# Row-wise infinity norm of an 8192x8192 matrix: the last 128 results transposed on VectorE and stored in four runs of 128 bytes

## The chip, the core and the metric

One core of a Trainium2 chip runs the kernel; the other seven stay idle. The metric is the device time of one execution in microseconds (us). The kernel before takes 626.61 us, the median of three runs that lie between 626.55 and 626.79.

Three parts of the core matter here. **DVE** (VectorE) computes the maxima. **SP** (SyncE) and **ACT** (ScalarE) do nothing but issue DMAs, each into a hardware queue of its own; 16 DMA engines carry the data of both. **POOL** (GpSimd) closes the program: it waits for the last transfers and resets the semaphores.

## What is computed

```python
x = randn(8192, 8192)                          # float32, 268 MB
out = np.linalg.norm(x, ord=np.inf, axis=1)    # 8192 float32
```

For a matrix, `ord=np.inf` with `axis=1` is the largest absolute value of each row. So every element is read once from HBM, and 32 KB are written.

## The kernel before, in words

The 8192 rows are 64 rows for each of the 128 partitions: 40 "bulk" rows and 24 "tail" rows.

**Bulk (L261 to L269).** 20 loads of 8 MB on SP, each two rows (16,384 elements) per partition, into a ring of three slots. One reduction on DVE per load writes two columns of `r_bulk`. A load waits until DVE has read the slot that it overwrites.

**Tail (L272 to L317).** Row r of the tail in partition p is DRAM row `split + 24 p + r` (`x_t`, L241), so 24 results lie side by side in each partition's output. The 24 rows are cut into 37 loads (`TAIL`, L20) that shrink from 16,384 to 512 elements per partition. A load may end inside a row. Then DVE reduces that piece to a partial maximum, which is put into a slot just ahead of the place in the ring where the row's last piece will land; the reduction of the last piece reads those slots with it (L307 to L313: `slot`, `frm`), and writes the row's column of `r_tail`. So the final reduction of a row depends on the reductions of all its pieces. The helper `absmax` (L252) records every reduction, so that all have line L253 in the profile.

The two last rows, 22 and 23, are loaded in alternation in 15 pieces (from the 22nd entry of `TAIL` on). The five last loads of the program are, in order: j = 32, a piece of row 23 (640 elements); j = 33, of row 22 (640); j = 34, of row 23 (512); j = 35, the last piece of row 22 (512); j = 36, the last piece of row 23 (512). Rows 22 and 23 have seven partials each, so that their final reductions read 519 elements.

**Stores.** When the reduction of load j = 34 is done (L314), ACT issues the store of `r_bulk` (L316): 640 runs of 32 bytes. After the last reduction SP issues the store of `r_tail` (L318): for each partition one run of 24 floats, 128 runs of 96 bytes in all.

**Order and waits.** The tile framework keeps the order of the code on each engine and adds semaphore waits. DVE counts its finished instructions in one semaphore; each DMA reports on one of eight semaphores ("lanes"), used in turn. `drop_implied_waits` (L134) takes away waits that others imply. An instruction that keeps two waits has the first of them in a small wait instruction of its own, ahead of it in the same queue. `finish_on_pool` (L71) rewrites the end: all engines meet at a barrier; POOL waits for the other lanes, clears the semaphores around the last store's lane, and then waits for that lane. Nothing of the program comes after that.

Of the kernel before, what the change touches and what calls it, by code (L numbers as in the profile page):

```python
# [12 lines left out]
F32 = mybir.dt.float32  # L13
# [3 lines left out]

HEAD, STEP = 32, 8

TAIL = [  # L20
# [10 lines left out]
]  # L31

# [178 lines left out]
@with_exitstack  # L211
def kernel(
    ctx: ExitStack,
    tc: tile.TileContext,
    x: bass.AP,
    out: bass.AP,
    G: int = 4,
    B: int = 2,
    SLOTS: int = 3,
    PAD: int = 128,  # L220
):
    nc = tc.nc
    P = nc.NUM_PARTITIONS
    rows, cols = x.shape
    W = B * cols
    R = SLOTS * W + PAD * 4


    n_tail = sum(w for _, w in TAIL) // cols
    met = 0  # L230
    for lo, w in sorted(TAIL):
        assert lo == met
        met += w
    assert met == n_tail * cols
    n_bulk_rows = rows // P - n_tail
    assert n_bulk_rows % (G * B) == 0
    A = n_bulk_rows // (G * B)
    split = n_bulk_rows * P
    x_b = x[:split].rearrange("(a p n b) c -> a n p (b c)", p=P, a=A, n=G, b=B)
    out_b = out[:split].rearrange("(a p n b) -> p a (n b)", p=P, a=A, n=G, b=B)  # L240
    x_t = x[split:].rearrange("(p t) c -> p (t c)", p=P)  # L241
    out_t = out[split:].rearrange("(p t) -> p t", p=P)

    pool = ctx.enter_context(tc.tile_pool(name="sbuf", bufs=1))
    r_bulk = pool.tile([P, A, G * B], F32)
    r_tail = pool.tile([P, n_tail], F32)
    used = [HEAD, A * G * B, n_tail]
    gap = -sum(-(-n // STEP) * STEP for n in used) % PAD
    pool.tile([P, gap], F32, name="gap")
    ring = pool.tile([P, R], F32)  # L250

    def absmax(o, i):  # L252
        return nc.vector.reduce_max(  # L253
            out=o, in_=i, axis=X, apply_absolute_value=True
        )

    def after(ins, first, kind):
        info = mybir.DependencyInfo(kind, mybir.DependencyReason.SCHED_ONLY)
        tc.add_manual_dep(ins.ins, first.ins.name, info, reason="order")

    for a in range(A):  # L261
        for n in range(G):
            at = (a * G + n) % SLOTS * W
            t = ring[:, at : at + W]
            nc.sync.dma_start(out=t, in_=x_b[a, n])
            absmax(
                r_bulk[:, a, n * B : (n + 1) * B],
                t.rearrange("p (b c) -> p b c", b=B),
            )  # L269


    pieces = []  # L272
    for j, (at, w) in enumerate(TAIL):
        end = at + w
        while at < end:
            r = at // cols
            to = min(end, (r + 1) * cols)
            pieces.append((j, r, to - at))
            at = to
    of_row = [[k for k, s in enumerate(pieces) if s[1] == r] for r in range(n_tail)]  # L280


    here = A * G % SLOTS * W
    start, slot = [], []
    for j, (_, w) in enumerate(TAIL):
        first = next(s for s in pieces if s[0] == j)
        ks = of_row[first[1]]
        n_part = len(ks) - 1 if pieces[ks[-1]][0] == j else 0
        at = -(-(here + n_part) // PAD) * PAD
        if at + w > R:  # L290
            at = -(-n_part // PAD) * PAD
        start.append(at)
        slot.append(at - n_part)
        here = at + w

    for j, (src, w) in enumerate(TAIL):
        at = start[j]
        nc.sync.dma_start(out=ring[:, at : at + w], in_=x_t[:, src : src + w])
        here = [k for k, s in enumerate(pieces) if s[0] == j]
        offs = [at + sum(pieces[i][2] for i in here[:m]) for m in range(len(here))]  # L300
        todo = list(zip(here, offs))
        if slot[j] != at:

            todo = todo[1:] + todo[:1]
        for k, lo in todo:
            _, r, n = pieces[k]
            ks = of_row[r]  # L307
            if k == ks[-1]:
                frm = slot[j] if len(ks) > 1 else lo
                done = absmax(r_tail[:, r : r + 1], ring[:, frm : lo + n])  # L310
            else:
                to = slot[pieces[ks[-1]][0]] + ks.index(k)
                done = absmax(ring[:, to : to + 1], ring[:, lo : lo + n])  # L313
        if j == len(TAIL) - 3:  # L314

            ins = nc.scalar.dma_start(out=out_b, in_=r_bulk[:])  # L316
            after(ins, done, mybir.DependencyClass.Sync)  # L317
    nc.sync.dma_start(out=out_t, in_=r_tail[:])  # L318
    nc.at_finalize(drop_implied_waits)
    nc.at_finalize(start_first_load_early)  # L320
    nc.at_finalize(finish_on_pool)
    nc.at_finalize(open_without_vector)
# [30 lines left out]
```

## Time and profile before

| | |
|---|---|
| median of three runs | 626.61 us (626.55 to 626.79) |
| the profiled execution's own time | 626.65 us |
| its span, first to last instruction of the program | 624.0 us |
| what lies around the span | 2.65 us |
| DVE busy | 553.1 us, 89% of the span |
| bytes read from HBM | 268.44 MB, mean 430 GB/s over the span |

How to read it: the span runs from the first instruction of the program to the last that an engine's instruction stream holds. A DMA that lands after that lies outside the span but inside the execution's time. "Busy" counts computing instructions alone; SP and ACT only issue DMAs and so have no busy time. In the chain, "issue" is time in which an engine waited for nothing that the profile shows, and a name with q (SPq, DVEq) is the sequencer of that engine, which waits, branches and issues DMAs.

### The profile page before, as it was taken

How to read it: one execution, taken by the hardware profiler on the slowest of the kernel's cores; microseconds unless marked ns; L12 is line 12 of the kernel's file. 1: busy time of each engine (PE TensorE's matmuls, PEld its weight loads, DVE VectorE, ACT ScalarE, POOL GpSimd, SP SyncE). 2: the span in 40 equal slices, each digit the busy share in tenths (PEclk: the TensorE clock that was granted, in tenths of full speed). 3: DMA queues.
4: the chain of work that ended last, by engine and by line, in shares of the span. 5: the costliest groups of instructions: out<-in, count | busy, mean ns of one | idle time of the engine just before them, and what ended most of it. 6: DMA issues, size and time to landing. Idle time of an engine off the chain costs nothing.

```text
span 624.0 us, 166 instructions
## 1 busy us (share of the span) xinstructions
DVE 553.1 (89%) x76; POOL 0.2 (0%) x4
## 2 busy tenths in 40 slices
DVE  0588988889988899888898888988899999999999
POOL 0000000000000000000000000000000000000000
DMA  9999999999999999999999999999999999999998
GB/s 403 454 420 454 420 441 433 408 466 403 471 403 454 420 454 420 450 424 429 445 408 466 403 466 408 454 420 454 409 435 445 422 436 428 429 427 431 429 425 343
DMA packets 8865, 268.47 MB, mean 430 GB/s; under 512 B 1568, under 2 KB 1568, under 8 KB 3488
## 3 DMA queue, kind: packets, MB, share of 16 engines
q1 hardware_dynamic: 8208, 268.44, 99.7%
q10 hardware_dynamic: 656, 0.02, 0.1%
q14 instruction: 1, 0.01, 0.0%
HBM read 268.44 MB, written 0.03 MB: 430 GB/s over the span
## 4 chain that ended last, share of the span: by engine, by line
DMA 61%; DVE 38%; issue 0%; DVEq 0%
DMA ring<-in_x_dram 61%; DVE r_bulk L253 19%; DVE ring L253 10%; DVE r_tail L253 9%; DVEq L348 0%
## 5 line engine op out<-in xcount | busy, mean ns | idle before, releaser
L253 DVE TENSOR_REDUCE r_bulk<-ring 128x2 f32<-128x16384 f32 x20 | 344.4, 17220 | 62.1 <-DMA ring<-in_x_dram 62.1
L253 DVE TENSOR_REDUCE r_tail<-ring 128x1 f32<-128x8192 f32 (+14 forms) x24 | 109.7, 4587 | 7.7 <-DMA ring<-in_x_dram 7.7
L253 DVE TENSOR_REDUCE ring<-ring 128x1 f32<-128x5248 f32 (+26 forms) x32 | 101.5, 3215 | 0.2 <-DMA ring<-in_x_dram 0.2
L337 POOL MEMSET const-bfloat16-1.0<- 128x1 bf16 x1 | 0.1, 101 | 0.0
L337 POOL MEMSET const-uint8-127<- 128x1 uint8 x1 | 0.1, 101 | 0.0
L337 POOL MEMSET const-float32-0.0<- 128x1 f32 x1 | 0.1, 98 | 0.2 <-issue 0.2
L337 POOL MEMSET const-float32-1.0<- 128x1 f32 x1 | 0.1, 98 | 0.0
## 6 DMA issues: line engine op xcount, KB each, us to landing
ring<-in_x_dram SPq DMA_DIRECT2D x1, 7744.0 KB, 39.6
ring<-in_x_dram SPq DMA_DIRECT2D x1, 7168.0 KB, 37.2
ring<-in_x_dram SPq DMA_DIRECT2D x1, 6400.0 KB, 33.0
ring<-in_x_dram SPq DMA_DIRECT2D x1, 5696.0 KB, 36.7
ring<-in_x_dram SPq DMA_DIRECT2D x1, 5056.0 KB, 41.0
ring<-in_x_dram SPq DMA_DIRECT2D x1, 4544.0 KB, 36.0
ring<-in_x_dram SPq DMA_DIRECT2D x1, 4032.0 KB, 31.9
ring<-in_x_dram SPq DMA_DIRECT2D x1, 3648.0 KB, 40.2
```

What stands on the lines that cost most here:

```text
L253: return nc.vector.reduce_max(out=o, in_=i, axis=X, apply_absolute_value=True)
L337: nc = _bacc.Bacc("TRN2", target_bir_lowering=False, num_devices=1)
```

## The change

All results now lie in one tile `r_all` of 64 columns: 40 of the bulk, then 24 of the tail. `r_bulk` and `r_tail` are views of it.

The last tail row (23) is no longer one of 24 adjacent rows per partition. It takes the last 128 rows of the matrix, one per partition (`x_l`, `out_l`); the other 23 tail rows are now 23 adjacent rows per partition. The loads of row 23 read from `x_l`, those of the others from `x_t` with 23 rows per partition.

The entries j = 34 and j = 35 of `TAIL` change places: first the last piece of row 22 (so row 22 is complete), then a piece of row 23; the last load, j = 36, stays.

The store of `r_bulk` on ACT is tied to the reduction of j = 33 instead of j = 34. A new store on ACT follows it: 23 tail columns, 128 runs of 92 bytes, once j = 34 has completed row 22.

After the last reduction DVE transposes columns 32 to 63 of `r_all`: each block of 32 partitions by 32 columns for itself. Column 63, the results of the last row, so becomes partitions 31, 63, 95 and 127 of `turned`, each with 32 results side by side. SP stores these four partitions: four runs of 128 bytes.

```diff
-    (194944, 640), (187264, 640), (195584, 512), (187904, 512),
+    (194944, 640), (187264, 640), (187904, 512), (195584, 512),
     (196096, 512),
...
-    x_t = x[split:].rearrange("(p t) c -> p (t c)", p=P)
-    out_t = out[split:].rearrange("(p t) -> p t", p=P)
+    n_lane = n_tail - 1
+    last = rows - P
+    x_t = x[split:last].rearrange("(p t) c -> p (t c)", p=P)
+    x_l = x[last:]
+    out_t = out[split:last].rearrange("(p t) -> p t", p=P)
+    out_l = out[last:].rearrange("(q i) -> q i", i=SQ)
...
-    r_bulk = pool.tile([P, A, G * B], F32)
-    r_tail = pool.tile([P, n_tail], F32)
-    used = [HEAD, A * G * B, n_tail]
+    n_bulk = A * G * B
+    assert n_bulk + n_tail >= SQ
+    r_all = pool.tile([P, n_bulk + n_tail], F32)
+    turned = pool.tile([P, SQ], F32)
+    r_bulk = r_all[:, :n_bulk].rearrange("p (a k) -> p a k", a=A)
+    r_tail = r_all[:, n_bulk:]
+    used = [HEAD, n_bulk + n_tail, SQ]
...
-        nc.sync.dma_start(out=ring[:, at : at + w], in_=x_t[:, src : src + w])
+        of, lo = (x_l, src - n_lane * cols) if src >= n_lane * cols else (x_t, src)
+        nc.sync.dma_start(out=ring[:, at : at + w], in_=of[:, lo : lo + w])
...
-        if j == len(TAIL) - 3:
-
-            ins = nc.scalar.dma_start(out=out_b, in_=r_bulk[:])
-            after(ins, done, mybir.DependencyClass.Sync)
-    nc.sync.dma_start(out=out_t, in_=r_tail[:])
+        if j == len(TAIL) - 4:
+
+            ins = nc.scalar.dma_start(out=out_b, in_=r_bulk)
+            after(ins, done, mybir.DependencyClass.Sync)
+        if j == len(TAIL) - 3:
+            nc.scalar.dma_start(out=out_t, in_=r_tail[:, :n_lane])
+    nc.vector.transpose(out=turned[:], in_=r_all[:, n_bulk + n_tail - SQ :])
+    nc.sync.dma_start(out=out_l, in_=turned[SQ - 1 :: SQ, :])
```

(`SQ` is 32.)

More of the change, by code (lines that the diff above doesn't have):

```diff
@@ L18 @@
 HEAD, STEP = 32, 8
+SQ = 32
 TAIL = [
```

## The prediction

> **What bounds the kernel now.** I read the page first, for the engines' shares and the chain.
>
> ```profile
> DVE 553.1 (89%) x76; POOL 0.2 (0%) x4
> ...
> DMA 61%; DVE 38%; issue 0%; DVEq 0%
> ```
>
> Loads and reductions share the chain, and only the stage at the end tells which of them a change there meets. So I read the end of the chain of waits (start, length, what):
>
> ```profile
> 533.82 39.07 DMA ring<-in_x_dram
> 572.89 0.02 issue
> 572.92 10.08 DVE ring L253 x2
> ...
> 606.33 15.17 DVE ring L253 x13
> 621.50 0.45 issue
> 621.95 0.14 DVE r_tail L253
> 622.09 0.36 issue
> 622.45 0.78 DVEq L348
> ```
>
> The last load that DVE waited for landed at 572.89. From there on reduction follows reduction: DVE is the bound for the last 50 us, and an instruction added there adds its whole cadence. But loads are close behind. By the trace's landings, the last ten loads land 0.14 to 0.27 us before their reductions start (the last at 622.41, its reduction starts at 622.55). So DVE could not gain much, and what delays DVE costs in full.
>
> The timeline has the last instructions, and the windows what the DMAs did meanwhile (length, DVE busy, POOL busy, clock, DMA share, GB/s):
>
> ```profile
> 621.36 0.68 DVE L253 TENSOR_REDUCE ring<-ring 128x1 f32<-128x512 f32 x1
> 621.95 0.68 DVE L253 TENSOR_REDUCE r_tail<-ring 128x1 f32<-128x519 f32 x1
> 622.55 0.68 DVE L253 TENSOR_REDUCE r_tail<-ring 128x1 f32<-128x519 f32 x1
> 622.07 0.41 ACTq L316 DMA_DIRECT2D out_dram<-r_bulk  x1
> 623.26 0.35 SPq L318 DMA_DIRECT2D out_dram<-r_tail  x1
> ```
> ```profile
> 621.00:622.00 1.00, 1.00 (x3) 0.00 (x0) 1.00 0.30 115
> 622.00:623.00 1.00, 1.00 (x3) 0.00 (x0) 1.00 0.01 2
> 623.00:624.00 1.00, 0.23 (x1) 0.00 (x0) 1.00 0.32 21
> 624.00:625.00 1.00, 0.00 (x0) 0.00 (x0) 1.00 0.09 12
> ```
>
> Each reduction starts 0.08 us before the end of the one before it (621.36 + 0.68 = 622.04 against 621.95). DVE ends at 623.23, SP issues the last store 0.03 later, and its packets move after 624. The view of DMA issues tells when stores land, in us from the issue:
>
> ```profile
> out_dram<-r_bulk ACTq DMA_DIRECT2D x1, 20.0 KB, 1.9
> out_dram<-r_tail SPq DMA_DIRECT2D x1, 12.0 KB, 1.4
> ```
>
> So the last store lands at 623.26 + 1.43 = 624.70, after the span's end (624.0), and POOL's last wait is for it. The profiled execution took 626.65 us, 0.04 above the median 626.61; from the landing to its end, with what lies ahead of the span, is 1.95 us, which I leave as it is. Three terms remain.
>
> **Term 1: two new waits of DVE on itself.** In the old order j = 34 was a piece of row 23 and j = 35 the end of row 22, so that each final reduction needed partials no younger than the reduction two places ahead. After the swap j = 34 completes row 22 and reads the partial that j = 33, just ahead, has written; j = 36 reads that of j = 35. The trace of before has no reduction that waits for its direct predecessor; I bound the cost. DVE's counter rises 0.01 us after an instruction's end, where the follower now starts 0.08 before it: at least 0.09 each. These reductions have two waits, so the counter's wait stands in an instruction of its own. In before such a one ran 0.028 us after its count (621.450, 621.478) and took 0.021; with 0.03 more for the start of the reduction (572.89 landed, 572.92 started, in the chain), the follower starts 0.01 + 0.03 + 0.02 + 0.03 = 0.09 after the predecessor's end instead of 0.08 ahead of it: 0.17 each. As the upper end I take 0.30 each: the fixed part of a reduction by a line through two rows,
>
> ```profile
> L253 DVE TENSOR_REDUCE ring<-ring 128x1 f32<-128x128 f32 x1 | 0.3, 275 | 0.0
> L253 DVE TENSOR_REDUCE r_tail<-ring 128x1 f32<-128x519 f32 x2 | 1.3, 683 | 0.0
> ```
>
> is 275 - 128 x (683 - 275)/391 = 141 ns, and it could be laid bare on top of the wait. Term 1: **+0.35** (0.18 to 0.60). Queued behind the waits on DVE are j = 35, j = 36 and the transpose; for the last of them waits SP's last store alone. Nothing hides it: the last load, landed at 622.41, is early already.
>
> The Trainium skill speaks against this term: "VectorE: DVE Perf Modes", section "The DRAIN you can't avoid", says that eight copies with a semaphore after each took as long as with one after the last, since the pipe empties between instructions anyway. The overlap of 0.08 us in the rows above disagrees. By the page the term would be 0, and the sum at most -0.02.
>
> **Term 2: the transpose.** One DVE instruction, 128x32, and SP now waits for it instead of for the last reduction. It waits for its direct predecessor, with one wait: 0.03, as above. Its length is in no row. The line above gives 141 + 32 x 1.04 = 175 ns for 32 columns; it writes 32 columns instead of one. Nearest row: the 128x128 reduction, 0.275. I take 0.24, then 0.01 for the counter: **+0.28** (0.17, with little fixed cost, to 0.58, the 0.545 of the 386-column reduction and the wait).
>
> **Term 3: the last store.** 4 runs of 128 bytes instead of 128 of 96. Of the 1.43 us, by the trace's packets: issue to first data packet 0.84, first to last data packet 0.21, from there to the last report 0.39. With four runs the 0.21 nearly goes: -0.19. For the 0.84, 640 runs (the r_bulk store) took 0.96 and 0.41 of issue against 0.35: 0.12 for 512 runs, so 124 fewer would save 0.03; the issue itself, if it is done engine by engine, would get shorter too, and single reports come together sooner: another 0.08 as a guess between nothing and the whole 0.35 of issue. Term 3: **-0.30**. Its ends: -0.50, where POOL's barrier and clearing (done at 624.11, 0.59 before the landing) become the bound, and +0.20, if few engines with one run each report later. The profile has no store that small.
>
> The Trainium skill, "DMA: Bandwidth & Descriptors", section "Why a DMA increments its semaphore by 16 and not by 1", says that such a DMA uses as many engines (up to 16) as divide both patterns' outermost size: here four. Its section "Anatomy of one DMA" puts most of a DMA's fixed time on the write receipt; by it the store would still take some 1.4 us, which is rival B. The trace has 0.39 of 1.43 behind the last data packet, which speaks for less.
>
> **At no cost.** The r_bulk store leaves ACT one reduction earlier (621.45 instead of 622.04). Its packets would run from about 622.43 (they came 0.96 after the issue) to 622.86, when the last load's have ended; if they slowed it, term 1 gives 0.46 us of cover (the last reduction now starts at about 622.87), and without cover they'd cost up to their 0.43. The new store of 23 columns is behind it on ACT, waits for row 22 (about 622.22), and lands near 623.7, before the last store's packets. SP's queue holds nothing but the last store. POOL has one more lane to wait for, landed by then: it hides in what is left of the 0.59 - 0.30; without that, 0.05. The swap moves no bytes: both loads have 512 columns.
>
> **Sum.** +0.35 + 0.28 - 0.30 = +0.33: 626.65 + 0.33 = 626.98 in the profiled execution, **626.94** against the median. That is 0.05%. A measurement of this kernel tells about 0.2% (1.25 us) from no change, so my forecast is no change, slightly on the slow side.
>
> **Rivals.**
> - **A, the store gains more than DVE loses.** Waits at 0.09 each, transpose 0.17, store -0.50: -0.15, 626.46. For it: 128 runs become four, and 0.35 of issue may shrink. Against: 0.84 and 0.39 of the old 1.43 have little to do with the number of runs. A fifth: 0.20.
> - **B, the store does not do what it is cut for** (lands 1.43 us after its issue, bound by its fixed parts): +0.35 + 0.28 = +0.63, 627.24. For it: the r_bulk store, five times as many runs, is only 0.5 us slower. 0.17.
> - **C, slower: the loads' new pitch.** Partitions of tail loads lie 23 rows (736 KB) apart instead of 24, those of the last row one row (32 KB). The tail moves 24 x 4.19 MB, some 234 us at 430 GB/s. If its rate falls by 1%, it ends 2.3 us later; less 0.2 us of slack, with the sum: 629.1. From 0.5% on (1.2 us) it decides by my bound. Against it: bulk loads at 256 KB and the first tail loads at 768 KB have the same cadence (19.31 us, and starts at 408.61, 427.90, 447.21), so a pitch has not mattered yet; for it: no row has a pitch that is no multiple of 256 KB. 0.07.
> - A faster rate of the loads can't bring much, DVE being the bound behind 572.9; with other gains 0.03 in all.
>
> Forecast 0.53, A 0.20, B 0.17, C 0.07, faster 0.03. The range takes the forecast, A and B with part of the bounds' far ends: 626.35 to 627.6, leaving out C and cases with all terms at one end (626.46 to 627.99 without C). Faster by over 0.2% 0.03, within 0.88, slower 0.09 (C, and terms that are all at their upper ends).
>
> **What would show it.** Term 1: starts of j = 34 and j = 36 about 0.09 us behind their predecessors' ends, not 0.08 ahead. Term 2: a transpose of 0.17 to 0.30 us, and SP's issue 0.63 later than 623.26, near 623.9. Term 3: a landing of the last store in 1.1 us; 1.4 is B, under 1.0 is A. C: DVE idle on loads after 573 us, or a slower cadence from 447 us on. I'm wrong if the last store's issue is later than 624.4 or its landing takes over 1.6.

## The result, and the profile after

The changed kernel takes **627.52 us**, the median of 22 runs (627.32 to 628.30), against 626.62 us (626.48 to 627.06) for the kernel before in 22 runs beside it: +0.90 us, or 0.14% of the median. The ratio estimated from all runs is 1.0016, with a 95% interval of 1.0009 to 1.0023. So the changed kernel is slower, clear of the noise. The ratio lies below the 0.2% that the prediction took as its bound (the interval reaches a little past it), and the loss is more than twice the 0.33 us that it forecast.

Some executions of every kernel, the one before too, take up to about 1 us longer than the fastest (in four traces of such executions the reduction of the 21st load starts 0.3 to 0.6 us later than in the trace of before), so the sizes below are read between instructions of one trace, and medians only confirm them.

Of the changed kernel there are two traces. Its first (an execution of 627.97 us) has on the page:

```profile
DVE 553.5 (88%) x77; POOL 0.2 (0%) x4
...
DMA 61%; DVE 38%; issue 0%; DVEq 0%
```

One more instruction on DVE, 0.4 us more of its time, and almost the same shares: nothing here shows 0.9 us. The end of the chain of waits does (start, length, what):

```profile
621.92 0.03 issue
621.94 0.02 DVEq L262
621.97 0.05 issue
622.01 0.69 DVE r_all L262
622.71 0.60 DVE ring L262
...
623.40 0.70 DVE r_all L262
624.11 0.02 issue
624.13 0.21 DVE turned L330
```

Ahead of the two final reductions (rows 22 and 23) now stands a gap in three parts: 0.03 from DVE's count to the wait instruction, 0.02 for that instruction (DVEq), and 0.05 until the reduction starts (ahead of the one at 623.40, among the lines left out, 0.03, 0.02 and 0.04). In before no such gap cost anything, since the count had come early enough (at 621.45, for the reduction that starts at 621.95). The timeline shows what follows:

```profile
622.74 0.36 ACTq L329 DMA_DIRECT2D out_dram<-r_all  x1
623.40 0.69 DVE L262 TENSOR_REDUCE r_all<-ring 128x1 f32<-128x519 f32 x1
624.13 0.21 DVE L330 STREAM_TRANSPOSE turned<-r_all 128x32 f32<-128x32 f32 x1
624.37 0.63 SPq L331 DMA_DIRECT2D out_dram<-turned  x1
```

The last line is the surprise: SP needs 0.63 us to issue four runs, where it issued 128 in 0.35. The windows (length, DVE busy, POOL busy, clock, DMA share, GB/s) show that nothing moves for a long time after that:

```profile
624.00:625.00 1.00, 0.31 (x2) 0.00 (x0) 1.00 0.00 0
625.00:626.00 1.00, 0.00 (x0) 0.00 (x0) 1.00 0.01 1
```

The store's first data packet starts 1.24 us after the issue began (before: 0.84), its last report comes at 1.64 (before: 1.43). The view of DMA issues has no landing time for it; the figure behind the size is missing:

```profile
out_dram<-turned SPq DMA_DIRECT2D x1, 0.5 KB
```

The trace has five updates of the store's semaphore by DMA in place of 16: one at 1.01 us after the issue began, before any data moves, and four reports from 1.57 to 1.64.

So the landing is read from the last of these reports. The account, first for the second trace (label after_again, an execution of 627.49 us): SP issues the last store at 623.90 instead of 623.26, +0.64: two waits 0.19 each and the transpose 0.26. The store lands 1.63 us later instead of 1.43, +0.19. Together +0.83; 627.49 - 626.65 is +0.84. In the first trace the same terms give 0.38 + 0.26 + 0.21 = 0.85, and another 0.46 us comes from far ahead of the change: the reduction of the 21st load starts 0.42 us later than in before (409.03 against 408.61), and the reduction that follows the last wait for a load starts 0.46 later (573.38 against 572.92). 0.85 + 0.46 = 1.31, against 627.97 - 626.65 = 1.32. The reductions of the 21st load in the timelines of before, of the first and of the second trace:

```profile
408.61 8.69 DVE L253 TENSOR_REDUCE r_tail<-ring 128x1 f32<-128x8192 f32 x1 [2.09 <-DMA ring<-in_x_dram]
409.03 8.69 DVE L262 TENSOR_REDUCE r_all<-ring 128x1 f32<-128x8192 f32 x1 [2.08 <-DMA ring<-in_x_dram]
408.53 8.69 DVE L262 TENSOR_REDUCE r_all<-ring 128x1 f32<-128x8192 f32 x1 [2.08 <-DMA ring<-in_x_dram]
```

### The profile page after: what moved, and what is told of

It reads as the page before. It is cut to its first block, busy times and chain, and to the rows that moved or that the text cites. A ratio compares the mean times of both kernels' runs of the same rounds, so it can differ in the third digit from the quotient of the medians.

```text
span 625.7 us, 169 instructions
## 1 busy us (share of the span) xinstructions
DVE 553.5 (88%) x77; POOL 0.2 (0%) x4
## 4 chain that ended last, share of the span: by engine, by line
DMA 61%; DVE 38%; issue 0%; DVEq 0%
DMA ring<-in_x_dram 61%; DVE r_all L262 28%; DVE ring L262 10%; DVE turned L330 0%; DVEq L262 0%
## 5 line engine op out<-in xcount | busy, mean ns | idle before, releaser
L262 DVE TENSOR_REDUCE r_all<-ring 128x2 f32<-128x16384 f32 (+15 forms) x44 | 454.1, 10329 | 70.5 <-DMA ring<-in_x_dram 70.3
```

Source lines behind the costliest of these rows:

```text
L262: return nc.vector.reduce_max(out=o, in_=i, axis=X, apply_absolute_value=True)
```

## The experiments

The theory at the start: the waits cost 0.19 us each, the transpose 0.26, the store 0.21 because it runs on few engines. Rivals: the loads' new layout; another property of the store. The first four kernels ran on one chip.

### The old order of the loads

```diff
-    (194944, 640), (187264, 640), (187904, 512), (195584, 512),
+    (194944, 640), (187264, 640), (195584, 512), (187904, 512),
...
-        if j == len(TAIL) - 3:
+        if j == len(TAIL) - 2:
             nc.scalar.dma_start(out=out_t, in_=r_tail[:, :n_lane])
```

> The swap of the two last-but-one loads is undone (the rest of the change stays; the store of 23 columns follows the reduction that then completes row 22). Theory (two waits of DVE on its own predecessor cost 0.19 us each, the transpose 0.26, the four-run store 0.21 more than the old one): the two final reductions again start 0.08 us before their predecessors' ends, and the time is 0.38 below the changed kernel's 627.5: 627.1. Rival (the loads' new layout makes it slower, not the waits): no change, 627.5.

Measured: 627.08 us (11 runs), ratio to the kernel before 1.0006 (0.9997 to 1.0015); the changed kernel on the same chip 627.47. The timeline:

```profile
621.18 0.67 DVE L262 TENSOR_REDUCE ring<-ring 128x1 f32<-128x512 f32 x1
621.77 1.28 DVE L262 TENSOR_REDUCE r_all<-ring 128x1 f32<-128x519 f32 x2
623.09 0.21 DVE L330 STREAM_TRANSPOSE turned<-r_all 128x32 f32<-128x32 f32 x1
623.33 0.63 SPq L331 DMA_DIRECT2D out_dram<-turned  x1
```

Two reductions of 0.68 us fill 1.28 us: they overlap by 0.08 again, and the one ahead too (621.18 + 0.67 against 621.77). By the medians the swap cost 0.39 us. The store's issue is as long as before this edit. What is left above the kernel before, 0.44 us, is the transpose (0.26) and the store (0.2); so the layout of the loads, which stays changed, costs nothing that shows.

### No transpose

```diff
-    out_l = out[last:].rearrange("(q i) -> q i", i=SQ)
+    out_l = out[last:].rearrange("(p t) -> p t", p=P)
...
-    nc.vector.transpose(out=turned[:], in_=r_all[:, n_bulk + n_tail - SQ :])
-    nc.sync.dma_start(out=out_l, in_=turned[SQ - 1 :: SQ, :])
+    nc.sync.dma_start(out=out_l, in_=r_tail[:, n_lane:])
```

> No transpose; the last store is 128 runs of 4 bytes, straight from the column of the last row. Theory (a store on four engines is issued and lands later than one on sixteen): issue 0.35 us instead of 0.63, landing 1.4 instead of 1.64 us after the issue, and 0.26 of the transpose gone: 627.5 - 0.21 - 0.26 = 627.05. Rival (short runs make the store late, whatever the number of engines): landing 1.6 or more, 627.25 or more.

Measured: 632.96 us (4 runs), ratio 1.0094 (1.0080 to 1.0108). The issue was 0.35 and the first data packet came 0.84 us after it, as the theory had it, but the view of DMA issues gives the landing as

```profile
out_dram<-r_all SPq DMA_DIRECT2D x1, 0.5 KB, 7.2
```

Neither side had that size: 128 runs of 4 bytes side by side land 6 us late. The last packet ends 1.04 us after the issue began; everything behind that is waiting for the reports, which come in one by one between 3.05 and 7.17 us. That is the store that the transpose avoids once the last row's results lie next to each other in HBM. The run says nothing against or for four engines.

### Sixteen runs on sixteen engines

```diff
-    out_l = out[last:].rearrange("(q i) -> q i", i=SQ)
+    out_l = out[last:].rearrange("(q i) -> q i", i=8)
...
-    nc.sync.dma_start(out=out_l, in_=turned[SQ - 1 :: SQ, :])
+    nc.sync.dma_start(out=out_l, in_=turned[7 :: 8, :8])
```

> As the changed kernel, but the last store takes 16 partitions of the transposed tile with 8 floats each: 16 runs of 32 bytes (the values stored there are not the results of the last rows). Theory (the number of engines decides): issue 0.35, landing 1.2 to 1.4 us after the issue, 627.05 to 627.3. Rival (a store of few runs is late because of what it writes): issue 0.6, landing 1.6, 627.5.

Measured: 627.52 us (11 runs), ratio 1.0010 (1.0002 to 1.0019).

The last store in the timeline:

```profile
623.88 0.55 SPq L331 DMA_DIRECT2D out_dram<-turned  x1
```

Sixteen engines report, and the issue is still 0.55 us, the landing 1.70. **The theory fell**: the number of engines does not make the issue long. (Four reports in the changed kernel and sixteen here are read as four engines and sixteen.)

### The changed kernel again

The kernel is not edited.

> The changed kernel once more, for a second trace. Theory (terms at the end add up to 0.84 us, and the 0.42 us by which the bulk loads of the first trace ended later belong to that execution): median 627.5, with most executions near 627.4, and a trace whose 21st load's reduction starts at 408.6 or at 409.0 by chance. Rival (the change delays the bulk loads): 0.4 us late again in the loads of 120 to 220 us.

Measured: 627.47 us (11 runs, 627.32 to 628.26), ratio 1.0012 (1.0003 to 1.0020). In its trace the reduction of the 21st load starts at 408.53, even ahead of before's 408.61. So the change does not by itself bring the 0.42 us of the first trace; the kernel before had executions above 627.1 on the same chip as well (7 of 27).

### Adjacent partitions

Two things were left for the store's issue: that its partitions are not adjacent (4 of them 32 apart, 16 of them 8 apart), or that they are fewer than 128. Three kernels part them; each has one of the three added lines, and none stores the results of the last rows.

```diff
-    nc.sync.dma_start(out=out_l, in_=turned[SQ - 1 :: SQ, :])
+    nc.sync.dma_start(out=out_l, in_=turned[:16, :8])      # adj16; out_l in 16 runs of 8
+    nc.sync.dma_start(out=out_l, in_=turned[:4, :])        # adj4
+    nc.sync.dma_start(out=out_l, in_=turned[1::2, :2])     # step64; out_l in 64 runs of 2
```

> As the changed kernel, but the last store takes 16 adjacent partitions with 8 floats each instead of 4 that lie 32 apart (the values stored are not the results of the last rows). Theory step (partitions that are not adjacent make the issue long): issue 0.35 instead of 0.55 to 0.63 us, first data packet 0.84 instead of 1.20 to 1.24 after the issue, landing 1.3; the time 0.3 below the changed kernel's 627.45: 627.15. Rival (a store of fewer than 128 partitions is issued on a longer path): issue 0.55, first packet 1.2, 627.5 as with 16 partitions 8 apart.

> As the changed kernel, but the four partitions of the last store are adjacent (0 to 3; not the results of the last rows). Theory step: issue at most 0.35 us, landing 1.3, 627.15. Rival (number of partitions): issue 0.63, first packet 1.24, landing 1.64, 627.45 as the changed kernel.

> As the changed kernel, but the last store takes every second partition, 64 of them with 2 floats each (not the results of the last rows). Theory step: issue 0.55 or more, first packet 1.2. Rival (number of partitions): an issue between the 0.35 of 128 partitions and the 0.55 of 16. Either way runs of 8 bytes land late, as the runs of 4 bytes did (7.2 us).

Measured: 627.21 us (10 runs) for 16 adjacent partitions, 627.14 (10 runs) for four (both with a ratio of 1.0007 to the kernel before, 0.9997 to 1.0016), one run of 629.12 for 64 partitions two apart. The changed kernel was not run on this chip, so the times alone do not settle it; the issues do. The lines of the last store in the timeline, in the same order:

```profile
624.36 0.36 SPq L331 DMA_DIRECT2D out_dram<-turned  x1
```
```profile
624.54 0.34 SPq L331 DMA_DIRECT2D out_dram<-turned  x1
```
```profile
623.98 0.54 SPq L331 DMA_DIRECT2D out_dram<-turned  x1
```

Adjacent partitions are issued in 0.34 to 0.36 us whether they are 4, 16 or 128; the 64, half of all, need 0.54. It is the distance, not the number. (By itself the 0.54 would fit the rival's range too; the adjacent 4 and 16 refute it.) (The late time of the third kernel is its landing, 3.2 us, with runs of 8 bytes side by side.)

### Runs of 4 bytes apart

The kernel before, with its last store split in two:

```diff
+        if j == len(TAIL) - 2:
+            nc.scalar.dma_start(out=out_t[:, : n_tail - 1], in_=r_tail[:, : n_tail - 1])
-    nc.sync.dma_start(out=out_t, in_=r_tail[:])
+    nc.sync.dma_start(out=out_t[:, n_tail - 1 :], in_=r_tail[:, n_tail - 1 :])
```

> The kernel before with its last store split: columns 0 to 22 leave on ACT once row 22 is complete, and SP stores column 23 alone, 128 runs of 4 bytes that lie 96 bytes apart (next to each other they landed in 7.2 us). Theory (neighbouring short runs wait for each other): issue 0.35, landing 1.4 to 2, 626.6 to 627.2. Rival (a run of 4 bytes is late by itself): landing near 7, 632.

Measured: one run of 626.67 us.

```profile
out_dram<-r_tail SPq DMA_DIRECT2D x1, 0.5 KB, 1.4
```

128 runs of 4 bytes that lie 96 bytes apart land in 1.42 us, against 7.2 side by side. So a run of 4 bytes is not late by itself; it is late beside others like it. (Runs of 32 bytes side by side, in the kernel with 16 adjacent partitions, landed in 1.35.) What makes such neighbours late is not shown. The run also shows that 128 runs of 4 bytes, far enough apart, gain nothing over 128 of 96 (1.43).

### The swap alone, and the transpose alone with adjacent partitions

The kernel before with the swap, and the changed kernel with the old order and four adjacent partitions:

```diff
-    (194944, 640), (187264, 640), (195584, 512), (187904, 512),
+    (194944, 640), (187264, 640), (187904, 512), (195584, 512),   # swap_only
...
-    nc.sync.dma_start(out=out_l, in_=turned[SQ - 1 :: SQ, :])
+    nc.sync.dma_start(out=out_l, in_=turned[:4, :])               # old_adj4
```

> The kernel before with nothing but the two entries of the list of loads swapped. Theory (two waits of DVE on its own predecessor, 0.19 us each): both final reductions start 0.10 to 0.11 us after their predecessors' ends, the last store is issued 0.38 later, 627.0 against 626.62; nothing else in the trace moves. Rival (the waits cost only beside the rest of the change): 626.6.

> The changed kernel with the old order of the loads and with four adjacent partitions in the last store (the values stored there are not the results of the last rows). Theory (terms add: transpose +0.26, waits 0, a four-run store from adjacent partitions 1.17 instead of 1.43 after its issue, -0.26): 626.6, no difference from the kernel before. Rival (adjacent partitions help only where the other stores have long landed): the store lands 1.4 after its issue, 626.9.

Measured: 627.03 us for the swap alone (11 runs), ratio 1.0003 (0.9994 to 1.0012), and 626.61 for the other (11 runs), ratio 0.9997 (0.9989 to 1.0006). The kernel before had a median of 626.97 on this chip, 626.44 at the lowest, so the swap's ratio alone does not tell 0.38 us from nothing. The trace of the swap shows the cost:

```profile
622.01 0.69 DVE L253 TENSOR_REDUCE r_tail<-ring 128x1 f32<-128x519 f32 x1
622.62 0.68 DVE L253 TENSOR_REDUCE ring<-ring 128x1 f32<-128x512 f32 x1
...
623.40 0.69 DVE L253 TENSOR_REDUCE r_tail<-ring 128x1 f32<-128x519 f32 x1
624.12 0.35 SPq L318 DMA_DIRECT2D out_dram<-r_tail  x1
```

The reduction at 622.62 overlaps its predecessor, those at 622.01 and 623.40 start 0.11 and 0.10 us behind theirs; that is 0.19 us lost for each of the two. In the second kernel the store from adjacent partitions lands 1.17 us after its issue and so gives back what the transpose costs (+0.26 and -0.26): no difference from the kernel before.

### Distance or first partition

All slow stores began at another partition than 0, all fast ones at 0. The last two kernels part these. The first of them puts the last row's results into column 0 of the tile and stores all results; both have the old order.

```diff
-    r_bulk = r_all[:, :n_bulk].rearrange("p (a k) -> p a k", a=A)
-    r_tail = r_all[:, n_bulk:]
+    r_bulk = r_all[:, 1 : n_bulk + 1].rearrange("p (a k) -> p a k", a=A)
+    r_tail = r_all[:, n_bulk + 1 :]
...
-                done = absmax(r_tail[:, r : r + 1], ring[:, frm : lo + n])
+                col = r_all[:, :1] if r == n_lane else r_tail[:, r : r + 1]
+                done = absmax(col, ring[:, frm : lo + n])
...
-    nc.vector.transpose(out=turned[:], in_=r_all[:, n_bulk + n_tail - SQ :])
-    nc.sync.dma_start(out=out_l, in_=turned[SQ - 1 :: SQ, :])
+    nc.vector.transpose(out=turned[:], in_=r_all[:, :SQ])
+    nc.sync.dma_start(out=out_l, in_=turned[::SQ, :])
```

The second has only this edit beside the old order:

```diff
-    nc.sync.dma_start(out=out_l, in_=turned[SQ - 1 :: SQ, :])
+    nc.sync.dma_start(out=out_l, in_=turned[31:35, :])
```

> The changed kernel with the old order of the loads; the results of the last row go to column 0 of the tile that is transposed, so that they stand in partitions 0, 32, 64 and 96 and the last store's four partitions begin at 0 (still 32 apart). All results are stored. Theory step (the distance of the partitions makes the issue long): issue 0.63, landing 1.64, 627.05 as with the old order alone. Rival start (it is long because the store begins at another partition than 0, as all long ones did): issue 0.35, landing 1.17, 626.6.

> The old order of the loads, and four adjacent partitions in the last store that begin at 31 instead of 0 (31 to 34; not the results of the last rows). Theory step: issue 0.35, landing 1.17, 626.6. Rival start: issue 0.63, landing 1.64, 627.05.

Measured: 627.05 us (11 runs, ratio 1.0006, 0.9997 to 1.0015) and one run of 626.55.

```profile
623.75 0.63 SPq L332 DMA_DIRECT2D out_dram<-turned  x1
```
```profile
623.42 0.35 SPq L331 DMA_DIRECT2D out_dram<-turned  x1
```

Partitions 32 apart that begin at 0 are issued in 0.63 us, adjacent ones that begin at 31 in 0.35: the distance it is. All last stores together, times in us from the start of the issue:

| last store | partitions | issue | first data packet | last report |
|---|---|---|---|---|
| before: 128 x 96 bytes | all | 0.35 | 0.84 | 1.43 |
| changed: 4 x 128 bytes | 32 apart, from 31 | 0.63 | 1.24 | 1.64 |
| start0: 4 x 128 bytes | 32 apart, from 0 | 0.63 | 1.23 | 1.63 |
| runs16: 16 x 32 bytes | 8 apart | 0.55 | 1.20 | 1.70 |
| step64: 64 x 8 bytes | 2 apart | 0.54 | 1.18 | 3.18 |
| adj16: 16 x 32 bytes | adjacent, from 0 | 0.36 | 0.85 | 1.35 |
| adj4: 4 x 128 bytes | adjacent, from 0 | 0.34 | 0.77 | 1.17 |
| adj4_from31: 4 x 128 bytes | adjacent, from 31 | 0.35 | 0.78 | 1.18 |
| no_turn: 128 x 4 bytes, side by side | all | 0.35 | 0.84 | 7.17 |
| apart: 128 x 4 bytes, 96 bytes apart | all | 0.35 | 0.84 | 1.42 |

No version here beats the kernel before. Of those with the transpose, only the ones that store adjacent partitions in the old order tie with it, and they do not store the last row's results: a transpose in blocks of 32 by 32 leaves these 32 apart.

## Why the prediction was right or wrong, step by step

- **Term 1, the waits: right.** Forecast 0.17 each, measured 0.19 (0.110 and 0.103 us behind the predecessor's end instead of 0.082 ahead). The working by single pieces (counter, wait instruction, start) is what the chain shows; the start took 0.04 to 0.05 instead of 0.03. The Trainium skill, "VectorE: DVE Perf Modes", section "The DRAIN you can't avoid", gives a measurement of eight copies in which the semaphores between them cost nothing extra; for these reductions that does not hold: the trace of swap_only shows 0.38 us for two waits, and the medians of old_order agree.
- **Term 2, the transpose: right.** Forecast 0.28, measured 0.26: 0.034 to start, 0.211 long, 0.01 for the counter. The length lies between the line through the reductions (0.175) and the guess of 0.24.
- **Term 3, the last store: wrong in sign.** Forecast -0.30 ("with four runs the 0.21 nearly goes", "the issue itself ... would get shorter too"), measured +0.19 to +0.21. The part about the runs was right: from adjacent partitions four runs land in 1.17 us, -0.26, with the spread of 0.21 down to 0.06 and the first packet earlier by 0.07; only the issue did not get shorter (0.34 against 0.35), so it does not go by the number of engines, as the guess of 0.08 supposed. What failed is the step that took the 0.84 from issue to first packet from stores whose partitions are adjacent. Partitions 32 apart make the issue 0.28 longer and the first packet 0.47 later (0.77 to 1.24); from there to the last report the two stores of four runs take the same 0.40. The edit's `turned[SQ - 1 :: SQ, :]` shows the distance; I looked at the number of runs and engines alone. The upper bound of +0.20 had the size by luck: its reason (few engines) is refuted by runs16, long with sixteen, and adj4, short with four.
- **Sum.** Forecast +0.33, measured +0.84 between undisturbed traces, +0.90 by medians; 0.5 of the difference is term 3. The direction came true, and with it a ratio within 0.2%, but the forecast of no change did not: with 22 runs on each side 0.9 us is clear of the noise, so the bound of 1.25 us was too coarse. That 627.52 lies in the range (up to 627.6) is luck, since the range reached that far for the sake of rival B and far ends with other reasons. The prediction's own sign of being wrong, a landing over 1.6 us, came in both traces (1.64 and 1.63).
- **Rival B** (the store gains nothing, 627.24) was the nearest; the store lost 0.2 us more than it allowed. **A** fell with term 3. **C**, the loads' pitch (the distance in HBM between the rows of two neighbouring partitions): refuted as far as these traces go; the first tail loads keep their cadence (starts at 409.03, 428.31 and 447.63 in the first trace), and in the second the last load lands at 622.38 against 622.41.
- **At no cost: right.** The two stores on ACT land at 623.84 and 624.19 in the first trace, ahead of the last store's packets (625.62), and the last load, landed at 622.87, waits 0.53 us for DVE. (The prediction's 622.87 for the start of the last reduction should be 622.90 by its own term 1, which gives 0.49 us of cover and not 0.46; nothing hangs on it.) POOL was nearly the bound: SP is ready for the barrier (its drain instruction ends) 1.11 us after it began to issue the store (before: 0.53), and POOL has cleared by 625.85, 0.16 before the landing, where I had counted on 0.29.

Why a distance between partitions makes SP's issue longer is not shown; the traces show only when the issue ends and when packets start. Also open is what lets the bulk loads of some executions end late; in the four traces where they do, it begins in the first 220 us, far ahead of the change, and executions as long occur in kernels with and without each part of it. In the trace of start0 (627.32 us) the bulk loads are not late (the 21st reduction starts at 408.55), and 0.23 us come later, among the loads of the tail (its last wait for a load ends at 573.15 against 572.92).

## What to carry to other kernels

Price a DMA by all of its access pattern, not by its bytes and runs: read what a store with *such* partitions costs from issue to first packet, and if the trace has none, let the range take a longer issue seriously. On an engine that is the bound, an instruction that reads what its direct predecessor wrote loses the overlap between the two (here 0.19 us); one other instruction in between gives it back for nothing. At the very end of a kernel every piece of the last store's latency counts in full, so measure the store alone before building work around it.

## What the runs showed of the hardware

- A store from partitions that are not adjacent (2, 8 or 32 apart) is issued in 0.54 to 0.63 us, one from adjacent partitions in 0.34 to 0.36 (4, 16 and 128 of them), both on SP. Its first data packet starts 1.18 to 1.24 us after the issue began, the other's after 0.77 to 0.85.
- 128 runs of 4 bytes side by side in HBM land 7.2 us after the issue, the same runs 96 bytes apart 1.42. 64 runs of 8 bytes side by side land in 3.2, 16 runs of 32 bytes side by side in 1.35.
- A DVE reduction that need not wait for the one just ahead starts 0.08 us before that one ends. One that waits for it through a wait instruction of its own starts 0.10 to 0.11 us behind its end; the transpose, whose wait stands in no instruction of its own, 0.03 behind.
- A store of four partitions reports four times, and one update comes ahead of them (1.01 us after the issue began in the changed kernel, 0.46 from adjacent partitions). The Trainium skill, "DMA: Bandwidth & Descriptors", section "Why a DMA increments its semaphore by 16 and not by 1", says that engines that take no part have their share of the count written at once by the issuing sequencer; five updates in place of 16 agree with that. Its section "Anatomy of one DMA — SWDGE (gpsimd) path" puts most of the fixed time of a DMA that GpSimd issues on the receipt of the write. The stores here, to which the prediction applied it, are issued by SP: in the one of 1.17 us from four adjacent partitions 0.77 lie ahead of the first data packet and 0.34 behind the last, so here the receipt is the smaller part.
